# Attention scores as two f32r products of 128 rows each: stacked queries, doubled keys, masks in f32r

## The chip, the cores and the metric

The kernel runs on one core of one Trainium2 chip. The metric is the device time of one execution in microseconds (us), taken from several runs; 2882.18 us is the median of three runs of the kernel before. One more execution was profiled, and every row below comes from it.

## The reference, cut to what matters

Three blocks follow each other on 256 rows of 1024 columns. The first and the third contain attention with 8 query heads of width 64; the second has none. What the change touches is the score of a query row against a key row, which is scaled, masked and put through a softmax:

```python
# first block, branch a (8 key heads), all 256 keys, causal
s_own = jnp.einsum('hqd,hld->hql', qc, k_own)
# first block, branch b (2 key heads): 15 compressed keys, then selected keys, then a window
s = jnp.einsum('grqd,gnd->grqn', qc, kc_b).astype(jnp.float32) * scale
s = jnp.einsum('grqd,gqnld->grqnl', qc, kg).astype(jnp.float32) * scale
s = jnp.einsum('grqd,gkd->grqk', qc, kwc).astype(jnp.float32) * scale
# third block, two layers (2 key heads): window of 128 and 16 meta rows, with a sink
s = jnp.einsum('bnqhgd,bnkhd->bnhgqk', qb, kw, preferred_element_type=jnp.float32) * (HEAD_DIM ** -0.5)
s = jnp.where(mask[None, :, None, None], s, -jnp.inf)
```

With 256 rows the selection and the window of branch b take in every earlier key, so the kernel computes both as causal attention over 256 keys. The layers of the third block see 272 rows in the first layer (16 meta rows are set ahead) and 256 query rows in the second.

## The kernel before, in words

All large products split both operands into a rounded part and a rest, in the type f32r, and add three products (`mm3`, lines 117 to 119): hi by hi, hi by lo, lo by hi. A weight chunk of 128 x 2048 is loaded by SP (`load`, line 108), rounded by ACT into `wh` (line 99) and its rest `wl` is taken by DVE (line 101), two halves each. TensorE (PE) works through these chunks, and the kernel places attention steps between them: `weave` and `gates` run one step of a large product (12 passes of 512 columns) for each step of attention.

Attention (`attend`, line 388) takes the 8 heads in four pairs, (0, 2), (1, 3), (4, 6), (5, 7). In round c it issues the scores of pair c, the product with the values of pair c-2 and the transposes of pair c-1. Queries and keys lie transposed, two heads above each other: head h has rows 64*(h%2) to 64*(h%2)+63 of `qT`. A score is a plain f32 product of 64 rows against 128 or 16 keys (line 409); a causal or window mask is added by a bf16 product of the identity and a mask tile (line 411):

```python
ps = k.tp((128, 2, 256))[:p]
k.pe = nc.tensor.matmul(ps[:, i, f:f + n], q(h), kt, start=True, stop=mask is None)
if mask is not None:
    nc.tensor.matmul(ps[:, i, f:f + n], identb[:p, :p], mask, start=False, stop=True)
```

DVE then takes the maximum (line 412) and ACT the exponential into a tile `P` (line 419), from the tag `w2k`, a ring of nine 2 KB tiles in the first block (`k.w2k, k.pt = 9, 4`, line 474) and of five in the third. `P` is turned by PE (line 428), copied to `PT` by DVE or ACT (lines 432, 434) and multiplied with the values (line 440).

In the first block `attend` runs for branch a (`moba`) and twice for branch b (`branches`), each for two tiles of 128 queries. Tile t=0 has one segment of 128 keys with a mask, t=1 has two segments of which the second has a mask. `cmp_scores` (line 642) adds 8 products of 64 rows against 15 compressed keys for each t (line 650). In the third block each layer has t=0 (128 keys with the causal mask, and the 16 meta keys with a mask), t=1 (two segments of 128 keys, each with a mask), and the first layer also t=2 (16 query rows against 16 keys).

The queries and keys reach `qT`, `kaT`, `kT2` and `kT` by four PE transposes and one ACT copy of 128 x 512 (lines 523, 1469). Between branch a and branch b stands `compress` (line 581), which builds the compressed keys and whose operands come from DVE.

Of the kernel before, what the change touches and what calls it, by code (L numbers as in the profile page):

```python
# [387 lines left out]
def attend(k, pool, p, q, segs, v, identb, sink=None):  # L388
# [10 lines left out]
    ns = [n for _, n, _ in segs(0)]  # L399
# [3 lines left out]
    def scores(c):  # L403
# [3 lines left out]
        for i, h in enumerate(hs):  # L407
            for f, (kt, n, mask) in zip(off, segs(h)):
                k.pe = nc.tensor.matmul(ps[:, i, f:f + n], q(h), kt, start=True, stop=mask is None)  # L409
                if mask is not None:  # L410
                    nc.tensor.matmul(ps[:, i, f:f + n], identb[:p, :p], mask, start=False, stop=True)  # L411
# [59 lines left out]
class Block1:  # L471
    def __init__(self, k, pool):
        self.k, self.pool = k, pool
        k.w2k, k.pt = 9, 4

    def consts(self):
# [7 lines left out]
        self.identb = pool.tile([128, 128], BF16, name="identb")  # L484
        nc.vector.tensor_copy(self.identb, k.ident)
        self.cmask = pool.tile([128, 128], BF16, name="cmask")
        nc.gpsimd.memset(self.cmask, 0.0)
        nc.gpsimd.affine_select(self.cmask, self.cmask, pattern=[[-1, 128]], base=0, channel_multiplier=1,
                                compare_op=OP.is_ge, fill=NEG)
        self.nmask = pool.tile([128, 2, 15], F32, name="nmask")  # L490
# [13 lines left out]
    def tiles(self):  # L504
        p = self.pool
        self.qT = {n: p.tile([128, 4, S], F32, tag="qT" + n, name="qT" + n) for n in "ab"}
        self.kaT = p.tile([128, 4, S], F32, tag="kaT", name="kaT")
        self.kT2 = p.tile([128, 4, S], F32, name="kT2")
        self.va = p.tile([128, 2, 512], F32, name="va")
        self.vs = p.tile([128, 2, 128], F32, name="vs")  # L510
        self.vw = p.tile([128, 2, 128], F32, name="vw")
        self.tT2 = p.tile([128, 4, S], F32, tag="tT2", name="tT2")
        self.gb = p.tile([128, 2, 24], F32, name="gb")
        self.mg = p.tile([128, 2, 2048], F32, name="mg")
        kdp = p.tile([128, 2, 4, 2, 64], F32, tag="kdp", name="kdp")
        self.kdp = [kdp[:, t] for t in range(2)]

    def heads_T(self, src, dst, t):
        k = self.k
        pt = k.tp()  # L520
        for i in range(4):
            k.nc.tensor.transpose(pt[:, i, :], src[:, i * 128:(i + 1) * 128], k.ident)
        k.nc.scalar.copy(dst[:, :, t * 128:(t + 1) * 128], pt)
# [14 lines left out]
    def group(self, j, t, ps):  # L538
        k, nc, pool = self.k, self.k.nc, self.pool
        self.flush(1)  # L540
        if j == 0:
            self.qk(t, ps, "a_q_g", self.qT["a"])
        elif j == 1:
            self.qk(t, ps, "a_k_g", self.kaT)
        elif j == 2:
            nc.scalar.copy(self.va[:, t], ps)
        elif j == 3:
            self.qk(t, ps, "b_q_g", self.qT["b"])
# [15 lines left out]
        else:  # L564
            self.kv2(t, ps[:, 0:128], "b_kw_g", 2)
            nc.scalar.copy(self.vw[:, t], ps[:, 128:256])
            self.heads_T_later(self.kdp[t].rearrange("p c a d -> p (c a d)"), self.kT2, t)
# [5 lines left out]
    def mgate(self, j, t, ps):  # L573
# [3 lines left out]
        m = self.mg[:, t, j * 512:(j + 1) * 512]  # L577
# [3 lines left out]
    def compress(self):  # L581
# [32 lines left out]
        self.kcT = pool.tile([128, 2, 15], F32, name="kcT")  # L614
# [19 lines left out]
        nc.scalar.copy(self.kcT, pt[:, 0:2, 0:15])  # L634

    def attend(self, t, qT, kT, v):
        return attend(self.k, self.pool, 128, lambda h: qT[64 * (h % 2):64 * (h % 2) + 64, h // 2, t * 128:(t + 1) * 128],
                      lambda h: [(kT(h // 2)[64 * (h % 2):64 * (h % 2) + 64, s * 128:(s + 1) * 128], 128,
                                  self.cmask if s == t else None) for s in range(t + 1)],
                      v, self.identb)  # L640

    def cmp_scores(self, t):
# [3 lines left out]
        for q in range(2):  # L646
            ps = k.tp((128, 4, 15))
            r = slice(64 * q, 64 * q + 64)
            for i in range(4):
                nc.tensor.matmul(ps[:, i, :], self.qT["b"][r, i, t * 128:(t + 1) * 128], self.kcT[r, i // 2, :],  # L650
                                 start=True, stop=True)
            nc.vector.tensor_tensor(s.rearrange("p (i q) n -> p q i n", q=2)[:, q], ps,
# [26 lines left out]
    def moba(self, t):  # L679
        k, nc, pool = self.k, self.k.nc, self.pool  # L680
        o, r = yield from self.attend(t, self.qT["a"], lambda hp: self.kaT[:, hp],
# [9 lines left out]
    def branches(self, t):  # L691
# [4 lines left out]
        steps = together(*(self.attend(t, self.qT["b"], lambda hp, i=i: self.kT2[:, 2 * i + hp // 2],  # L696
# [24 lines left out]
    def merge(self):  # L721
        k, nc, pool = self.k, self.k.nc, self.pool
        M = [k.xn() for t in range(2)]
        for h in range(2):
            ch = [k.stream(k.a["w_up_" + n][h, 0]) for n in "ab"]
            c = slice(h * 512, h * 512 + 512)
            for i, n in enumerate("ab"):
                for t in range(2):
# [6 lines left out]
                    gate = self.mg[:, t, i * 1024 + h * 512:i * 1024 + h * 512 + 512]  # L735
# [9 lines left out]
    def run(self):  # L745
# [25 lines left out]
        tags = {"ah": "qTa", "al": "kaT", "bh": "tT2", "bl": "kdp"}  # L771
        yT = lambda n: [pool.tile([128, 4, S], F32R, tag=tags[n + i], name="y" + n + i) for i in "hl"]
        self.yT = {"a": yT("a")}
# [13 lines left out]
        self.yT["b"] = yT("b")  # L787
# [584 lines left out]
class Block3:  # L1372
# [3 lines left out]
    def __init__(self, k, wc):  # L1376
# [10 lines left out]
        self.identb = tl("identb3", [128, 128], BF16)  # L1387
        nc.vector.tensor_copy(self.identb, k.ident)
        self.mask = {}
        for n, base, cm, st, w in (("causal", 0, 1, -1, 128), ("far", -1, -1, 1, 128), ("meta", 111, -1, 1, 16)):  # L1390
            m = self.mask[n] = tl("m" + n, [128, w], BF16)
            nc.gpsimd.memset(m, 0.0)
            nc.gpsimd.affine_select(m, m, pattern=[[st, w]], base=base, channel_multiplier=cm,
                                    compare_op=OP.is_ge, fill=NEG)

# [27 lines left out]
    def meta_cols(self, mt, xx, k0, k1):  # L1423

        self.k.nc.scalar.copy(mt[:, k0:k1, 0:META], xx[:, 0, k0:k1, S:])
        self.k.nc.vector.tensor_copy(mt[:, k0:k1, 32:32 + META], xx[:, 1, k0:k1, S:])
# [26 lines left out]
    def qkv(self, l, pool, nt):  # L1453
# [3 lines left out]
        self.qT = tl("qT", [128, 4, SM])  # L1457
        self.kT = tl("kT", [128, 2, SM])
# [3 lines left out]
        def flush(keep=0):  # L1462

            while len(later) > keep:
                src, n, dst, P = later.pop(0)
# [3 lines left out]
                nc.scalar.copy(dst, pt[:, :n, :P])  # L1469
# [3 lines left out]
        for t in (0, 1, 2):  # L1473
            for j, (w, N) in enumerate(ws):
# [14 lines left out]
                if j == 0:  # L1489
# [3 lines left out]
                    later.append((q.rearrange("p h d -> p (h d)"), 4, self.qT[:, :, o:o + P], P))  # L1493
                else:
# [6 lines left out]
                    later.append((kd.rearrange("p g a d -> p (g a d)"), 2, self.kT[:, :, o:o + P], P))  # L1501
# [3 lines left out]
    def attention(self, l, t, sink, g):  # L1505
# [3 lines left out]
        kt = lambda h, s, n: self.kT[64 * (h % 2):64 * (h % 2) + 64, h // 4, s * 128:s * 128 + n]  # L1509
        M = self.mask  # L1510
        sl = {0: ((0, 128, M["causal"]), (2, 16, M["meta"])),
              1: ((0, 128, M["far"]), (1, 128, M["causal"])),
              2: ((2, 16, M["causal"][:META, :META]),)}[t]
        o, r = yield from attend(k, pool, P, lambda h: self.qT[64 * (h % 2):64 * (h % 2) + 64, h // 2, t * 128:t * 128 + P],
                      lambda h: [(kt(h, s, n), n, m) for s, n, m in sl],
                      lambda s, h: self.v[:sl[s][1], sl[s][0], h // 4 * 64:h // 4 * 64 + 64], self.identb, sink)
# [9 lines left out]
        k.split(self.yy[:, 0, 0:4, c], self.yy[:, 1, 0:4, c], pt[:, :, :P])  # L1526

    def conv(self, l, nt):
# [50 lines left out]
        yield  # L1579
        for cb in range(4):  # L1580
            z = u[:, cb, :n0]
            nc.vector.scalar_tensor_tensor(z, z, self.cg[:, cb:cb + 1], rb, op0=OP.mult, op1=OP.mult)
            k.split(self.yy[:, 0, 4 + cb, :n0], self.yy[:, 1, 4 + cb, :n0], z)
# [46 lines left out]
    def mix(self, l, nt):  # L1630
        k, nc, a = self.k, self.k.nc, self.k.a
        with ExitStack() as ctx:
# [11 lines left out]
            self.yy = pool.tile([128, 2, 8, SM], F32R, name="yy")  # L1644
# [12 lines left out]
            def normalised():  # L1657
                for _ in conv:
                    pass
                if nt == 3:  # L1660
                    self.meta_cols(my, self.yy, 4, 8)
            if nt == 3:
                self.meta_cols(my, self.yy, 0, 4)
            g2, gn = k.row(None, src=a["mix_post_g"][l]), k.row(None, src=a["mlp_pre_g"][l])
            w = a["w3_out"][l]
            yy = lambda c: (self.yy[:, :, 2 * c:2 * c + 2], None if my is None else my[:, 2 * c:2 * c + 2])
# [174 lines left out]
def body(tc, a, out):  # L1841
    with ExitStack() as ctx:
# [6 lines left out]
        with ExitStack() as c:  # L1849
            k.work(c, 2, 2)  # L1850
# [30 lines left out]
```

## Time and profile before

| what | value |
|---|---|
| median of three runs (lowest to highest) | 2882.18 us (2879.19 to 2885.19) |
| the profiled execution's own time | 2877.76 us |
| its span, first to last instruction | 2875.4 us |
| PE busy | 97% of the span |
| DVE, ACT, POOL busy | 61%, 47%, 10% |
| mean granted TensorE clock | 0.978 |

The span is the time from the first to the last instruction on the core; 2.4 us of the execution's own time lie around it. The clock is a share of full speed: it has two levels, 2.4 GHz (1.00) and 1.2 GHz (0.50), so 0.66 over ten us means some 7 us at the lower level. A matmul's recorded duration contains its latency, and passes overlap; the time that a pass takes from the stream is the distance from its start to the start of the next. A plain f32 product leaves two MATMUL records.

### The profile page before, as it was taken

The numbers are of one execution on the slowest core, as the hardware profiler recorded it, in microseconds if no ns is written. First come the engines' busy times: TensorE is split into PE (matmuls) and PEld (weight loads), VectorE is DVE, ScalarE is ACT, GpSimd is POOL, SyncE is SP. The second block draws the span as 40 slices with busy tenths as digits, with TensorE's granted clock in tenths as the row PEclk, the third lists the DMA queues.
The fourth block names the chain that finished last, engine by engine and source line by source line (L and its number), as shares of the span: only waits on it lengthen the run. The fifth ranks groups of instructions, "written<-read, shape, count | busy, mean of one in ns | idle before, by whom it ended". The sixth has DMA issues, their size and how long they took to land. (4 is left out here: it accounts for less than half of the span.)

```text
span 2875.4 us, 44682 instructions
## 1 busy us (share of the span) xinstructions
PE 2779.6 (97%) x18212; PEld 2497.4 (87%) x18212; DVE 1767.7 (61%) x2983; ACT 1351.4 (47%) x2278; POOL 288.8 (10%) x308
## 2 busy tenths in 40 slices
PE   8999979999999999999999999999999999999999
PEld 6787979989999888988799898888988888888897
DVE  6646799775555556548855554766546464464654
ACT  4544445544444555435544444434445354453543
POOL 2101640000000000004300000241001100000100
PEclk9999999999999999999999999999999999998999
DMA  5424437896665555554255555434554234442452
GB/s 205 169 78 148 148 133 261 287 309 217 215 204 202 195 196 203 191 187 152 81 205 190 190 180 188 165 110 162 183 191 163 70 132 161 156 152 74 161 191 103
DMA packets 105982, 496.75 MB, mean 173 GB/s; under 512 B 11040, under 2 KB 44320, under 8 KB 50224
## 3 DMA queue, kind: packets, MB, share of 16 engines
q1 hardware_dynamic: 61632, 443.15, 44.2%
q10 hardware_dynamic: 44144, 50.74, 5.3%
q8 instruction: 143, 2.34, 0.3%
q14 instruction: 63, 0.52, 0.0%
HBM read 476.03 MB, written 17.83 MB: 172 GB/s over the span
## 5 line engine op out<-in xcount | busy, mean ns | idle before, releaser
L101 DVE TENSOR_TENSOR wl<-raw,wh 128x1024 fp32r<-128x1024 f32 x808 | 971.1, 1223 | 636.2 <-ACT wh L99 635.3
L99 ACT CAST wh<-raw 128x1024 fp32r<-128x1024 f32 x848 | 862.1, 1041 | 727.6 <-PE acc L118 239.1
L118 PE MATMUL acc<-xx,wh 128*128 128x256 f32 x1504 | 424.4, 282 | 0.0
L117 PE MATMUL acc<-xx,wh 128*128 128x256 f32 x1504 | 424.0, 282 | 0.0
L119 PE MATMUL acc<-xx,wl 128*128 128x256 f32 x1504 | 423.9, 282 | 0.0
L117 PE MATMUL tp<-xx,wh 128*128 128x256 f32 (+1 forms) x1440 | 410.6, 285 | 5.6 <-ACT ga L970 5.6
L119 PE MATMUL tp<-xx,wl 128*128 128x256 f32 (+1 forms) x1440 | 408.6, 284 | 2.1 <-DVE wl L101 2.1
L118 PE MATMUL tp<-xx,wh 128*128 128x256 f32 (+1 forms) x1440 | 408.5, 284 | 0.0
L117 PEld LDWEIGHTS acc<-xx,wh 128*128 128x128 f32 x1504 | 285.6, 190 | 0.3 <-ACT xs L278 0.3
L119 PEld LDWEIGHTS acc<-xx,wl 128*128 128x128 f32 x1504 | 285.6, 190 | 0.0
L118 PEld LDWEIGHTS acc<-xx,wh 128*128 128x128 f32 x1504 | 283.6, 189 | 0.0
L117 PEld LDWEIGHTS tp<-xx,wh 128*128 128x128 f32 x1440 | 274.0, 190 | 9.1 <-ACT ga L970 6.1
L118 PEld LDWEIGHTS tp<-xx,wh 128*128 128x128 f32 x1440 | 274.2, 190 | 2.4
L119 PEld LDWEIGHTS tp<-xx,wl 128*128 128x128 f32 x1440 | 273.6, 190 | 2.5 <-DVE wl L101 2.5
L117 PE MATMUL acc<-wh,xx 128*128 128x256 f32 (+2 forms) x672 | 226.4, 338 | 3.0 <-ACT xx L112 3.0
L118 PE MATMUL acc<-wl,xx 128*128 128x256 f32 (+2 forms) x672 | 221.9, 331 | 4.1 <-DVE wl L101 4.1
L119 PE MATMUL acc<-wh,xx 128*128 128x256 f32 (+2 forms) x672 | 219.8, 330 | 1.2 <-DVE xx L113 1.2
L147 POOL TENSOR_SCALAR va<-ss 128x1 f32<-128x1 f32 (+1 forms) x49 | 24.5, 500 | 1954.3 <-ACT junk L143 1770.9
L987 PE MATMUL o<-wl,wth 128*128 128x512 f32 x512 | 200.0, 391 | 1.9 <-DVE wl L101 1.9
L986 PE MATMUL o<-wh,wth 128*128 128x512 f32 x512 | 200.6, 392 | 0.0
L989 PE MATMUL o<-wh,wtl 128*128 128x512 f32 x512 | 159.7, 390 | 0.0
L117 PEld LDWEIGHTS acc<-wh,xx 128*128 128x128 f32 x672 | 131.0, 195 | 14.6 <-ACT xx L112 5.0
(483 smaller groups left out, 4817.9 us busy)
## 6 DMA issues: line engine op xcount, KB each, us to landing
raw<-in_ffn_in_dram SPq DMA_DIRECT2D x88, 1024.0 KB, 4.8
raw<-in_peer_u_dram SPq DMA_DIRECT2D x64, 1024.0 KB, 5.0
raw<-in_peer_v_dram SPq DMA_DIRECT2D x64, 1024.0 KB, 4.8
raw<-in_ffn_out_dram SPq DMA_DIRECT2D x44, 1024.0 KB, 4.8
raw<-in_w_up_dram SPq DMA_DIRECT2D x32, 1024.0 KB, 4.8
raw<-in_w_down_dram SPq DMA_DIRECT2D x32, 1024.0 KB, 4.8
gd<-gt ACTq DMA_DIRECT2D x16, 1024.0 KB, 5.5
G<-gd ACTq DMA_DIRECT2D x16, 1024.0 KB, 8.1
```

The costliest lines, as they stand in the source:

```text
L99: nc.scalar.copy(h[:, c], r[:, c])
L101: eng.tensor_tensor(l[:, c], r[:, c], h[:, c].bitcast(F32), op=OP.subtract)
L117: mm(out, ah, bh, start=start, stop=False)
L118: mm(out, ah, bl, start=False, stop=False)
L119: mm(out, al, bh, start=False, stop=stop)
L147: nc.gpsimd.tensor_scalar(v, ss[:, 0:1], EPS, ss[:, 1:2], op0=OP.add, op1=OP.add)
L986: mm(acc[t][h], wh, vh[:, h], start=st, stop=False)
L987: mm(acc[t][h], wh, vl[:, h], start=False, stop=False)
L989: mm(acc[t][h], wl, vh[:, h], start=False, stop=sp)
```

## The change

A query is now kept as hi and lo above each other: `qT` becomes 128 rows x 8 heads, rows 0 to 63 the part rounded to f32r, rows 64 to 127 the rest. The keys stand twice: the tile hi holds the rounded keys in both halves, the tile lo the rest of the keys in rows 0 to 63 and zeros in rows 64 to 127. One pass of 128 rows against hi gives (q_hi + q_lo) by k_hi, one against lo gives q_hi by k_lo. Segments that lie next to each other are one pass: 256 keys at t=1. The masks and the identity become f32r, and the mask passes stand between the pass against hi and the one against lo. The splitting is done when the transposes leave PSUM. To make room, `w2k` goes from 9 to 7 tiles and `pt` from 4 to 3 in the first block, and `mg`, `yT` and, in the third block, half of `yy` move into tiles whose work is over; the ring of 1024-wide gain rows goes from 2 to 1 in the first block.

```diff
+def split_queries(k, pool, Q, pt, c):
+    n = pt.shape[-1]
+    hi = pool.tile([128, 4, 128], F32R, tag="w2k", name="qh", bufs=k.w2k)[:, :, :n]
+    k.nc.scalar.copy(hi, pt)
+    heads = Q.rearrange("p (i e) s -> p e i s", e=2)
+    for e in range(2):
+        r = slice(64 * e, 64 * e + 64)
+        k.nc.vector.tensor_tensor(heads[64:128, e, :, c], pt[r], hi[r].bitcast(F32), op=OP.subtract)
+        k.nc.scalar.copy(heads[0:64, e, :, c], hi[r].bitcast(F32))
+def split_keys(k, hi, lo, pt):
+    k.nc.scalar.copy(hi, pt)
+    k.nc.vector.tensor_tensor(lo[0:64], pt[0:64], hi[0:64].bitcast(F32), op=OP.subtract)
+def score(k, out, Q, hi, lo, mask=None):
+    k.pe = k.nc.tensor.matmul(out, Q, hi, start=True, stop=False)
+    if mask:
+        mask()
+    k.nc.tensor.matmul(out, Q, lo, start=False, stop=True)
...
-            for f, (kt, n, mask) in zip(off, segs(h)):
-                k.pe = nc.tensor.matmul(ps[:, i, f:f + n], q(h), kt, start=True, stop=mask is None)
-                if mask is not None:
-                    nc.tensor.matmul(ps[:, i, f:f + n], identb[:p, :p], mask, start=False, stop=True)
+            f = 0
+            for hi, lo, n in segs(h):
+                def mask():
+                    for at, m in masks:
+                        if f <= at < f + n:
+                            nc.tensor.matmul(ps[:, i, at:at + m.shape[-1]], identr[:p, :p], m, start=False, stop=False)
+                score(k, ps[:, i, f:f + n], Q[:, h, c0], hi, lo, mask)
+                f += n
...
-        k.w2k, k.pt = 9, 4
+        k.w2k, k.pt = 7, 3
...
+        for x in (self.kaL, self.kT2[1]):
+            self.k.nc.gpsimd.memset(x[64:128].bitcast(F32), 0.0)
...
+    def put_ka(self, pt, c):
+        for e in range(2):
+            r, o = slice(64 * e, 64 * e + 64), slice(64 - 64 * e, 128 - 64 * e)
+            k.nc.scalar.copy(hi[r, e, :, c], pt[r])
+            k.nc.scalar.copy(hi[o, e, :, c], pt[r])
+            k.nc.vector.tensor_tensor(lo[0:64, e, :, c], pt[r], hi[r, e, :, c].bitcast(F32), op=OP.subtract)
...
-            ps = k.tp((128, 4, 15))
+            ps = k.tp((128, 4, 16))
             for i in range(4):
-                nc.tensor.matmul(ps[:, i, :], self.qT["b"][r, i, t * 128:(t + 1) * 128], self.kcT[r, i // 2, :],
-                                 start=True, stop=True)
+                score(k, ps[:, i, :], self.qT["b"][:, 2 * i + q, t * 128:t * 128 + 128], *(x[:, i // 2] for x in self.kcT))
...
-            m = self.mask[n] = tl("m" + n, [128, w], BF16)
+            m = wc.tile([128, 128], F32, tag="mask", name="mask")[:, :w]
...
+            self.mask[n] = tl("m" + n, [128, w], F32R)
+            nc.vector.tensor_copy(self.mask[n], m)
...
-        sl = {0: ((0, 128, M["causal"]), (2, 16, M["meta"])),
-              1: ((0, 128, M["far"]), (1, 128, M["causal"])),
-              2: ((2, 16, M["causal"][:META, :META]),)}[t]
+        runs, masks, sl = {0: (((0, 128), (S, META)), ((0, M["causal"]), (128, M["meta"])), ((0, 128), (2, META))),
+                           1: (((0, 256),), ((0, M["far"]), (128, M["causal"])), ((0, 128), (1, 128))),
+                           2: (((S, META),), ((0, M["causal"][:META, :META]),), ((2, META),))}[t]
```

How the instructions stand on the engines, before and after. First PE, in the first block, round 0 of branch a: the four heads whose scores stand ahead of the first woven step (two heads of t=0, two of t=1). `kaT`, `kaH`, `kaL` are the keys, `qTa` the queries, `tp` the scores in PSUM. Before:

```order
L409 MATMUL tp<-kaT,qTa 128x128
L411 LDWEIGHTS identb
L411 MATMUL tp<-cmask,identb 128x128
L409 MATMUL tp<-kaT,qTa 128x128
L411 LDWEIGHTS identb
L411 MATMUL tp<-cmask,identb 128x128
L409 MATMUL tp<-kaT,qTa 128x128 x2
L411 LDWEIGHTS identb
L411 MATMUL tp<-cmask,identb 128x128
L409 MATMUL tp<-kaT,qTa 128x128 x2
L411 LDWEIGHTS identb
L411 MATMUL tp<-cmask,identb 128x128
```

With the change, the same four heads:

```order
L410 MATMUL tp<-kaH,qTa 128x128
L441 MATMUL tp<-cmask,identr 128x128
L413 MATMUL tp<-kaL,qTa 128x128
L410 MATMUL tp<-kaH,qTa 128x128
L441 MATMUL tp<-cmask,identr 128x128
L413 MATMUL tp<-kaL,qTa 128x128
L410 MATMUL tp<-kaH,qTa 128x256
L441 MATMUL tp<-cmask,identr 128x128
L413 MATMUL tp<-kaL,qTa 128x256
L410 MATMUL tp<-kaH,qTa 128x256
L441 MATMUL tp<-cmask,identr 128x128
L413 MATMUL tp<-kaL,qTa 128x256
```

Every head now has three products, two of them 256 columns wide at t=1; the place in PE's order is the same, ahead of the same twelve passes.

Second, PE in the third block, one head of t=0 in the first layer. Before:

```order
L409 MATMUL tp<-kT,qT 128x128
L411 LDWEIGHTS identb_21180
L411 MATMUL tp<-mcausal,identb_21180 128x128
L409 MATMUL tp<-kT,qT 128x16
L411 LDWEIGHTS identb_21180
L411 MATMUL tp<-mmeta,identb_21180 128x16
```

With the change:

```order
L410 MATMUL tp<-kTh,qT 128x128
L441 MATMUL tp<-mcausal,identr 128x128
L413 MATMUL tp<-kTl,qT 128x128
L410 MATMUL tp<-kTh,qT 128x16
L441 MATMUL tp<-mmeta,identr 128x16
L413 MATMUL tp<-kTl,qT 128x16
```

This head has six products, three of them of 16 columns.

Third, DVE between branch a and `compress`, behind the last products of branch a. `hss` and `hn` belong to the norm of the last keys of branch b, `Xs` is an operand of `compress`, `gb` a gate. Before:

```order
L368 TENSOR_REDUCE hss<-xn 128x2
L101 TENSOR_TENSOR wl<-raw,wh 128x1024
L371 TENSOR_TENSOR hn<-acc,qy 128x128
L113 TENSOR_TENSOR Xs<-Xc,Xs 128x480
L372 TENSOR_TENSOR hn<-hn,row 128x128
L570 TENSOR_SCALAR gb<-gb 128x24
```

With the change:

```order
L397 TENSOR_TENSOR qTb<-tp,qh 64x4x128 x2
L368 TENSOR_REDUCE hss<-xn 128x2
L404 TENSOR_TENSOR kT2l<-tp,kT2h 64x4x128
L371 TENSOR_TENSOR hn<-acc,qy 128x128
L113 TENSOR_TENSOR Xs<-Xc,Xs 128x480
L372 TENSOR_TENSOR hn<-hn,row 128x128
L621 TENSOR_SCALAR gb<-gb 128x24
```

Three subtractions of 64 x 512 now stand ahead of `Xs` in DVE's order, and a fourth (`kT2l` of the second tile) further down.

## Rows read from the trace of the kernel before

**Rows 1.** The page: the span, and busy time by engine.

```profile
span 2875.4 us, 44682 instructions
PE 2779.6 (97%) x18212; PEld 2497.4 (87%) x18212; DVE 1767.7 (61%) x2983; ACT 1351.4 (47%) x2278; POOL 288.8 (10%) x308
```

**Rows 2.** Windows, the attention stages: length, busy by engine (instructions), PEclk, DMA, GB/s.

```profile
57.00:224.00 167.00, 160.08 (x970) 130.23 (x969) 97.22 (x215) 79.33 (x192) 9.85 (x14) 0.96 0.33 116
2190.00:2285.00 95.00, 94.81 (x631) 81.52 (x630) 51.81 (x124) 44.12 (x111) 6.12 (x7) 0.93 0.39 137
2550.00:2660.00 110.00, 108.79 (x671) 95.89 (x670) 62.59 (x123) 48.55 (x108) 9.79 (x15) 0.89 0.36 125
```

**Rows 3.** Waits of PE in 2180:2340, the largest: total, times, longest.

```profile
PE tp L205 <- DVE xn L165: 3.5, 2, 1.8
```

**Rows 4.** Timeline of PE, first block: start, duration, line, tiles, shape, count.

```profile
57.51 0.48 PE L409 MATMUL tp<-kaT,qTa 64*128 64x128 f32 x2
...
58.09 0.49 PE L409 MATMUL tp<-kaT,qTa 64*128 64x128 f32 x2
...
58.66 0.71 PE L409 MATMUL tp<-kaT,qTa 64*128 64x128 f32 x4
...
59.46 0.71 PE L409 MATMUL tp<-kaT,qTa 64*128 64x128 f32 x4
```

**Rows 5.** Timeline of PE, compressed scores of the first block.

```profile
179.53 1.20 PE L650 MATMUL tp<-kcT,qTb 64*128 64x15 f32 x13
...
181.12 0.23 PE L411 MATMUL tp<-cmask,identb 128*128 128x128 bf16 x1
```

**Rows 6.** Timeline of PE, third block, masks of t=0 and t=1.

```profile
2235.98 0.23 PE L411 MATMUL tp<-mcausal,identb 128*128 128x128 bf16 x1
...
2237.00 0.23 PE L411 MATMUL tp<-mcausal,identb 128*128 128x128 bf16 x1
...
2266.86 0.23 PE L411 MATMUL tp<-mfar,identb 128*128 128x128 bf16 x1
...
2268.01 0.23 PE L411 MATMUL tp<-mfar,identb 128*128 128x128 bf16 x1
```

**Rows 7.** Timeline of PE: passes of 128, 64 and 256 columns in a stream.

```profile
113.87 1.04 PE L205 MATMUL tp<-ident,ya 128*128 128x128 f32 x8
...
223.01 1.06 PE L440 MATMUL acc<-vw,PT 128*128 128x64 f32 x8
...
2196.10 0.28 PE L117 MATMUL acc<-wh,xx 128*128 128x256 f32 x1
...
2197.16 0.28 PE L117 MATMUL acc<-wh,xx 128*128 128x256 f32 x1
```

**Rows 8.** Windows inside the attention stages, for the clock: columns as in rows 2.

```profile
57.00:100.00 43.00, 43.00 (x256) 34.97 (x255) 23.25 (x58) 20.42 (x58) 5.45 (x8) 1.00 0.28 93
138.00:196.00 58.00, 57.83 (x325) 45.88 (x326) 28.94 (x68) 25.15 (x71) 0.00 (x0) 0.90 0.29 100
2230.00:2260.00 30.00, 30.00 (x170) 26.29 (x171) 11.56 (x30) 8.00 (x28) 0.92 (x2) 0.77 0.21 71
2580.00:2640.00 60.00, 60.00 (x349) 52.35 (x348) 27.07 (x58) 18.82 (x49) 0.79 (x2) 0.80 0.31 106
```

**Rows 9.** Lines 113 and 112: durations in ns (min/median/max), first and last start.

```profile
L113 DVE TENSOR_TENSOR xx<-tp,xx x59: 271/682/693, 12.3 to 2695.2; 128x512 fp32r<-128x512 f32 x56, 128x128 fp32r<-128x128 f32 x3
...
L112 ACT CAST xx<-tp x59: 266/587/600, 11.5 to 2693.7; 128x512 fp32r<-128x512 f32 x56, 128x128 fp32r<-128x128 f32 x3
```

**Rows 10.** Windows where new work may not be covered: columns as in rows 2.

```profile
30.00:60.00 30.00, 27.80 (x126) 21.97 (x124) 20.77 (x34) 13.22 (x20) 6.53 (x6) 0.94 0.49 174
100.00:120.00 20.00, 14.76 (x118) 12.77 (x117) 18.54 (x48) 13.70 (x23) 3.53 (x4) 1.00 0.55 189
```

**Rows 11.** Timeline of DVE and ACT: one pair of heads, maximum to exponential.

```profile
58.77 0.42 DVE L412 TENSOR_REDUCE nm<-tp 128x2 f32<-128x256 f32 x1
...
59.85 0.36 ACT L419 ACTIVATE P<-tp,nm 128x128 f32<-128x128 f32 x1
```

## What the change would do to the time, before it was run

> **What bounds the kernel now.** The page comes first: PE is busy for 97% of the span, DVE for 61%, ACT for 47%, POOL for 10% [rows 1]. That is a mean over stages, so the windows of the three stages with attention are read next [rows 2]. PE is busy for 160.1 of 167 us, 94.8 of 95 and 108.8 of 110; DVE for 55 to 58%, ACT for 44 to 48%. The waits of PE say the same from the other side: the largest of the third block's first attention stage comes to 3.5 us in all, on a norm and not on attention [rows 3]. So PE's stream sets the time here, and a microsecond of score passes saved is a microsecond of the span, as long as DVE and ACT deliver. One more thing stands in rows 2: the granted clock was 0.96, 0.93 and 0.89. With levels of 1.0 and 0.5, the time at the lower one is twice the missing share: 2 x 0.04 x 167 + 2 x 0.07 x 95 + 2 x 0.11 x 110 = 51 us.
>
> The sum is made against the profiled execution, 2877.8 us (span 2875.4 us [rows 1] and 2.4 us around it). It lies 4.4 us, or 0.15%, under the median of 2882.2 us; I take differences from it and set them on the median. A measurement of this kernel can tell about 0.2%, some 5.8 us, from no change: between 2876.4 and 2887.9 us counts as the same.
>
> **The scores before.** The price is the distance between starts. In the first block two heads of t=0 start 0.58 us apart and two of t=1 0.80 us apart [rows 4]. Three attentions of 8 heads make 24 heads for each t: 24 x 0.58 = 13.9 us and 24 x 0.80 = 19.2 us. The compressed scores begin 1.59 us ahead of the next mask; some 0.55 us of that are passes of the next scores, issued between them, so 1.04 us for each t, 2.1 us in all [rows 5]. In the third block equal masks of neighbouring heads are 1.02 us apart at t=0 and 1.15 us at t=1 [rows 6]; two layers make 16 heads for each: 16.3 and 18.4 us. Together 69.9 us at full clock.
>
> **The scores after.** A pass of f32r with 256 columns costs 0.118 us (nine passes from 2196.10 to 2197.16), and a pass in f32 of 128 columns 0.11 us (eight in 1.04 us, less the latency of one) [rows 7]. A pass of 64 columns takes 0.11 us as well [rows 7], so at these widths it isn't the columns that set the distance. No f32r pass of 128 columns stands in this trace. Bounds from its neighbours: half of the 256-column pass below, 0.059 us; two passes of plain f32 above, 0.22 us, since the two more passes of a t=1 head make 0.80 - 0.58 us [rows 4]. I take 0.11 us, the row of equal width and one pass. That gives, head by head:
> - first block, t=0: three passes, 24 x 0.33 = 7.9 us; t=1: two wide and a mask, 24 x (0.236 + 0.11) = 8.3 us;
> - compressed: 32 passes of 16 columns, 3.5 us; here the change loses 1.4 us, as products of the two 64-row halves run beside each other today (13 records in 1.20 us [rows 5]) and no longer do;
> - third block, t=0: six passes, 16 x 0.66 = 10.6 us; t=1: two wide and two masks, 16 x 0.456 = 7.3 us.
>
> Together 37.6 us, so **32.3 us saved**. Part of it is fewer passes; the rest is the delay at each step between 64-row f32 and 128-row bf16, which three-product heads of one shape don't have: two passes and a mask at 0.11 us would be 0.33 us and take 0.58 us [rows 4]. The eight heads of 16 query rows in the third block have three small passes before and after; I set them at nothing.
>
> If a 128-column pass took 0.10 us, 280 passes would save 3 us more; if some of the delay stayed at the steps to the passes around the scores, 5 us less: 27 to 37 us.
>
> **The clock.** Branch a's stretch, 57 to 100 us, runs at 1.00; the losses are at 138 to 196 us (0.90), 2230 to 2260 (0.77) and 2580 to 2640 (0.80) [rows 8], where scores of two attentions stand together. These three hold 49 of the 51 us at the lower level. Work there takes twice its time, so some 25 us is all that the clock could give back. The new scores are little more than half as long, and they are the part of these stretches that changes; but the transposes and products with values (64 and 128 columns at 0.11 us, as slack as before) stay. I take 10 us back, less than half, and 0 to 20 as the bounds: not all can come back while these stay, and below nothing I see no reason, as more of each stretch becomes wide passes.
>
> **What DVE and ACT get.** In the first block each of 2 query sets, 2 tiles gives two subtractions of 64 x 512 and branch a's keys two more for each tile, the doubled keys one: 14. The nearest price is 0.68 us for 128 x 512 (a 64-row one may be no cheaper): 9.5 us of DVE [rows 9]. ACT gets some 14 half copies at up to 0.59 us, 8.3 us [rows 9]. The third block gets about 12 more of each. Against windows at 55 to 58% of DVE and 44 to 48% of ACT [rows 2] this is hidden in the mean. Two places are thin. At 100 to 120 us DVE is busy for 18.5 of 20 us and PE for 14.8 only [rows 10]: four subtractions there, three ahead of the operand that `compress` waits for, come to 2.7 us on the path. At 30 to 60 us DVE has 9.2 us free [rows 10], the eight subtractions of branch a want 5.4 of them: 1 us. The third block's masks now pass one buffer three times, with a cast on DVE between, ahead of the norm that PE already waited 3.5 us for [rows 3]: 1 us. The memsets go to POOL, 10% busy [rows 1], and the smaller rings are the rival below: nothing else. **5 us**, between 0 (all in gaps) and 12 (all 14 subtractions and the masks half in the open).
>
> **The sum.** 2882.2 - 32.3 - 10 + 5 = **2845 us**. Ends: 2882 - 37 - 20 + 0 = 2825 and 2882 - 27 - 0 + 12 = 2867.
>
> **The rivals.**
> - *Narrow f32r passes run like plain f32.* 176 of the new passes have 128 columns: 96 in the first block at t=0, t=1's masks among them, 48 at t=0 and 32 masks at t=1 in the third. At 0.22 instead of 0.11 us they cost 19.4 us more: **2864 us**; with the costs at their upper end 2871. For it: plain f32 takes two passes, and nothing in the trace shows f32r under 256 columns. Against it: at 256 columns f32r takes one pass at 0.118 us. Chance 0.20.
> - *The clock gives nothing back.* The stretches that fell keep their other short passes: **2855 us**. Chance 0.13.
> - *Narrow passes run closer than 0.11 us*, since the same queries are the weights of two passes in a row and their load may be prepared beside the mask: at the middle between 0.059 and 0.11 us, 280 passes of up to 128 columns save 7 us more: **2838 us**. Against it: all of rows 7 under 256 columns stand at 0.11. Chance 0.05. The Trainium skill, page "TensorE: Matmul & The Clock Gate", section "Back-to-back issue gap", gives about 81 ns for each matmul of 128 columns in a sustained stream; by that the sum would be 280 x 0.029 = 8 us lower, and the trace does not agree, as its passes of 128 and of 64 columns stand 110 ns apart [rows 7].
> - *Slower: the ring of tiles becomes the bound.* `w2k` has 7 tiles for 9 in the first block, and the new `qh` takes from it. If the exponential must wait for the transposes of an older `P`, PE gets each round's transposes late by the chain from maximum to exponential, 58.77 to 60.21 us, 1.45 us [rows 11]. With 12 rounds in the first block and 20 in the third, 32 x 1.45 = 46 us, against 32.3 + 10 - 5 = 37 saved: **2891 us**. It decides once more than seven tiles (five in the third block) are wanted at once; two attentions together hold some two `P` each and a finished row, five. Chance 0.04.
> - *The change doesn't do what it says*: steps between row layouts stay, or work in the open takes most of the saving, near **2880 us**. Chance 0.06.
>
> **How the numbers follow.** The forecast has 0.52, the rivals 0.20, 0.13, 0.05, 0.04 and 0.06. All but the last two lie between 2826 and 2872 us; those two hold 0.10, and some of the others' tails the rest of 2 in 10. Faster by over 0.2% are the forecast and the first three rivals but for a tail of the first, 0.88; the same 0.07; slower 0.05, the ring and its like.
>
> **What the profile after would show.** In the first block, starts of scores at t=0 0.33 us apart by head, at t=1 0.35; 0.55 or more would be the first rival. The windows at 138 to 196 us and at the two places of the third block with a clock over 0.90, or unchanged ones for the second. PE's idle time around 100 to 120 us up by some 3 us, its waits on `Xs` and on the third block's norm longer by about 1 us. An ACT exponential waiting on PE's transposes in every round would be the ring. The forecast is wrong if scores with their masks take more than 50 us at full clock, or if the stages are shorter by more than scores and clock explain.

## The result, and the profile after

The kernel with the change takes 2855.28 us at the median of six executions, the kernel before 2879.64 us, at a ratio of 0.9926 with a 95% interval of 0.9910 to 0.9941, so 17 to 26 us less. The 2879.64 us are the median of six executions, three of them those of the first table; the ratio comes out of the other three (2872.94, 2874.50 and 2880.08 us), so it lies nearer to 1 than the quotient of the two medians, 0.9915. One of the six executions of the kernel with the change took 6404.74 us, for a reason that nothing here shows, and is left out of the ratio. The change is faster by more than 0.2%, as forecast. The time is 10 us above the forecast of 2845 us, and of the 37 us that were forecast to go, some 21 by the ratio have gone. The profiled execution fell from a span of 2875.4 to 2851.1 us, by 24.3 us.

The page of the kernel after, its head:

```profile
span 2851.1 us, 44585 instructions
PE 2744.9 (96%) x18132; PEld 2481.8 (87%) x18132; DVE 1786.7 (63%) x3018; ACT 1364.5 (48%) x2302; POOL 294.8 (10%) x314
```

The windows of rows 2 and rows 10 again, with the columns of rows 2:

```profile
57.00:224.00 167.00, 153.32 (x914) 131.63 (x913) 104.88 (x225) 86.33 (x202) 9.41 (x14) 0.91 0.34 118
2190.00:2285.00 95.00, 93.04 (x668) 82.73 (x666) 60.00 (x143) 48.84 (x123) 9.24 (x13) 0.98 0.42 142
2550.00:2660.00 110.00, 104.09 (x693) 94.59 (x692) 70.01 (x139) 54.14 (x114) 13.66 (x17) 0.95 0.38 129
100.00:120.00 20.00, 14.73 (x97) 12.65 (x97) 16.13 (x45) 13.06 (x25) 3.57 (x6) 0.83 0.47 159
30.00:60.00 30.00, 26.34 (x120) 20.56 (x119) 23.58 (x39) 16.91 (x24) 8.21 (x6) 1.00 0.44 161
```

The three attention stages have parted. In the window of the first block PE is busy for 153.3 us instead of 160.1, and that isn't a saving: it stands idle for the rest, and its clock fell from 0.96 to 0.91. In the third block the clock rose from 0.93 and 0.89 to 0.98 and 0.95 [rows 2].

The table divides both spans at the same passes of PE (the 205th, the 3109th and the 3701st of line 118; both kernels have 3872). Scores are counted from the start of each of their passes to the start of the next one on PE, without idle time between the two, and at full clock: time at the lower level counts half. Idle is time in which no pass runs. The clock's part is half the time at the lower level.

| before to after, us | length | scores | PE idle | clock | other passes |
|---|---|---|---|---|---|
| first block | 233.0 to 235.8 | 32.7 to 21.6 | 19.2 to 28.7 | 8.5 to 15.4 | 172.5 to 170.3 |
| between | 1946.9 to 1943.4 | none | 54.1 to 53.3 | 27.3 to 23.9 | 1865.5 to 1866.3 |
| third block | 549.5 to 526.2 | 34.3 to 20.7 | 15.7 to 17.5 | 23.9 to 11.9 | 475.7 to 476.1 |
| end | 146.1 to 145.7 | none | 6.9 to 6.9 | 2.3 to 2.3 | 136.9 to 136.5 |
| sum of the differences | -24.3 | -24.8 | +10.4 | -8.6 | -1.3 |

So the first block spends 11.1 us less on scores and ends 2.8 us later, while the third block gains 23.3 us, more than the 13.6 us that its scores save. These are two single executions, and the clock's part differs between executions of one kernel. An estimate from each execution's span and granted clock (span times the missing share) gives a mean loss to the clock of 58.9 us in 41 executions of the kernel before and of 53.6 us in five with the change: 5 us of gain by the clock, and 17 us by the rest.

The timeline of PE in the kernel after, two heads of t=0 in the first block and what follows them, then a head of t=0 and two of t=1 in the third block:

```profile
73.04 0.33 PE L410 MATMUL tp<-kaH,qTa 128*128 128x128 f32 x1
73.21 0.27 PE L441 MATMUL tp<-cmask,identr 128*128 128x128 f32 x1
73.32 0.28 PE L413 MATMUL tp<-kaL,qTa 128*128 128x128 f32 x1
73.43 0.28 PE L410 MATMUL tp<-kaH,qTa 128*128 128x128 f32 x1
...
73.77 0.61 PE L472 MATMUL acc<-va,PT 128*128 128x64 f32 x4
...
2237.11 0.33 PE L410 MATMUL tp<-kTh,qT 128*128 128x128 f32 x1
...
2237.80 0.31 PE L410 MATMUL tp<-kTh,qT 128*128 128x128 f32 x1
...
2262.97 0.37 PE L410 MATMUL tp<-kTh,qT 128*128 128x256 f32 x1
2263.18 0.23 PE L441 MATMUL tp<-mfar,identr 128*128 128x128 f32 x1
2263.24 0.27 PE L441 MATMUL tp<-mcausal,identr 128*128 128x128 f32 x1
2263.35 0.34 PE L413 MATMUL tp<-kTl,qT 128*128 128x256 f32 x1
2263.52 0.28 PE L410 MATMUL tp<-kTh,qT 128*128 128x256 f32 x1
```

Inside a head the 128-column passes stand 0.11 us apart (73.21, 73.32, 73.43). Behind a 256-column pass one of them takes less, 0.06 us (2263.18 to 2263.24). The heads of the third block take 0.69 us at t=0 (2237.11 to 2237.80) and 0.55 us at t=1 (2262.97 to 2263.52), where 0.66 and 0.46 were forecast, and the pair from 73.04 to 73.77 takes 0.73 us, not 2 x 0.33. The kernel before shows the opposite, a pair within other passes:

```profile
63.10 0.49 PE L409 MATMUL tp<-kaT,qTa 64*128 64x128 f32 x2
...
64.16 0.39 PE L428 MATMUL tp<-ident,P 128*128 128x128 f32 x2
```

1.06 us, not 2 x 0.58: the last mask (at 64.09 us) is left after 0.07 us, as the next pass follows at once.

The new idle time of the first block, 9.4 us, is spread. Counted between the same passes of line 118, 1.2 us of it are added up to the 25th pass, 1.5 up to the 49th, 3.5 up to the 85th (branch a), 2.9 up to the 121st (between branch a and `compress`) and 0.4 behind. In branch a, where the kernel before has no wait of PE at all, PE now waits for the softmax and for a norm; its largest waits in 57:94 of the kernel after:

```profile
PE tp L460 <- ACT P L451: 1.3, 1, 1.3
PE tp L558 <- DVE hn L385: 1.2, 1, 1.2
PE acc L472 <- DVE PT L466: 1.1, 2, 0.9
PE tp L410 <- ACT P L451: 0.8, 1, 0.8
```

Between branch a and `compress` PE waited before as well. The waits in 94:140, before and then after:

```profile
PE acc L117 <- ACT Xs L112: 2.2, 1, 2.2
PE tp L522 <- DVE kdp L536: 2.1, 2, 1.2
PE acc L119 <- DVE Xs L113: 1.0, 2, 0.8
```

```profile
PE tp L558 <- DVE kdp L587: 3.4, 1, 3.4
PE acc L117 <- ACT Xs L112: 2.6, 1, 2.6
PE acc L119 <- DVE Xs L113: 1.4, 2, 1.1
PE tp L205 <- DVE qTb L397: 0.8, 1, 0.8
```

The waits for the keys (`kdp`) and for the split queries (`qTb`), both of DVE, grew by 2.1 us together, those for `Xs` by 0.4 us on ACT and 0.4 on DVE. How late `Xs` is shows in the timeline, the last addition on DVE that it needs and then ACT:

```profile
105.44 0.58 DVE L644 TENSOR_TENSOR Xc<-tT,pos 128x240 f32<-128x240 f32 x1
...
109.91 0.60 ACT L393 CAST qh<-tp 128x512 fp32r<-128x512 f32 x1
...
110.56 1.24 ACT L398 CAST qTb<-qh 64x512 fp32r<-64x512 f32 x2
111.81 0.59 ACT L112 CAST Xs<-Xc 128x480 fp32r<-128x480 f32 x1
```

`Xs` could be cast from 106.0 us on and is cast at 111.8, behind the second tile's queries in ACT's order; its rest on DVE, behind the subtractions, follows at 115.3. Before, ACT waited for the data and cast them at once:

```profile
102.25 0.59 ACT L112 CAST Xs<-Xc 128x480 fp32r<-128x480 f32 x1 [1.12 <-DVE Xc L593]
```

At the very start there is a cost of another kind. The timeline of DVE before, then those of DVE and of POOL in the kernel after:

```profile
8.76 0.88 DVE L165 TENSOR_SCALAR xn<-xn,ya 128x512 f32<-128x512 f32 x2 [1.14 <-POOL ya L150]
```

```profile
8.94 2.51 DVE L165 TENSOR_SCALAR xn<-xn,ya 128x512 f32<-128x512 f32 x2 [1.20 <-POOL ya L150]
11.38 2.35 DVE L101 TENSOR_TENSOR wl<-raw,wh 128x1024 fp32r<-128x1024 f32 x2
...
9.07 2.10 POOL L545 MEMSET kaL<- 64x2048 f32 x1
...
12.70 0.95 POOL L545 MEMSET kT2l<- 64x1024 f32 x1
```

The same two scalings took 0.88 us before; now they take 2.51 us and end soon after POOL's memset of 2.10 us.

### The profile page after: what moved, and what is told of

Read it like the earlier page. It is cut to its first block, busy times and chain, and to the rows that moved or that the text cites. A ratio compares the mean times of both kernels' runs of the same rounds, so it can differ in the third digit from the quotient of the medians.

```text
span 2851.1 us, 44585 instructions
## 1 busy us (share of the span) xinstructions
PE 2744.9 (96%) x18132; PEld 2481.8 (87%) x18132; DVE 1786.7 (63%) x3018; ACT 1364.5 (48%) x2302; POOL 294.8 (10%) x314
## 4 chain that ended last, share of the span: by engine, by line
PE 63%; issue 23%; DVE 7%; POOL 3%; ACT 3%; DMA 1%; POOLq 0%; ACTq 0%; DVEq 0%
PE acc L119 6%; PE acc L117 6%; PE acc L118 6%; PE tp L119 4%; PE tp L117 4%; PE tp L118 4%; PE o L1037 4%; PE o L1036 4%; PE o L1039 4%; PE o L316 2%; PE o L317 2%; PE o L319 2%; DVE wl L101 1%; PE o L1667 1%; PE o L1664 1%
## 5 line engine op out<-in xcount | busy, mean ns | idle before, releaser
L147 POOL TENSOR_SCALAR va<-ss 128x1 f32<-128x1 f32 (+1 forms) x49 | 24.3, 496 | 1949.8 <-ACT junk L143 1768.1
L118 PEld LDWEIGHTS acc<-wl,xx 128*128 128x128 f32 x672 | 132.2, 197 | 16.7 <-DVE wl L101 6.9
```

Of the source, the lines that this page charges most:

```text
L118: mm(out, ah, bl, start=False, stop=False)
```

## The experiments

Each is told against the change as it stands ("the whole change", ratio 0.9926). The intervals of single kernels are some 0.15% wide to either side, about 4 us.

**Which block pays.** The classes of the two blocks, exchanged one at a time for those of the kernel before (the edits in words, as they are long):

```diff
-Block1 and attend of the change          # third_only
+Block1 and attend of the kernel before
-Block3 and attend of the change          # first_only
+Block3 and attend of the kernel before
```

> The third block has the new scores, the first block the old ones. Theory: the whole gain is made in the third block, where the two traces differ by 22 us, and the first block gives its saving back; so this kernel is as fast as the whole change or a little faster, 20 to 25 us under the kernel before, a ratio of 0.991 to 0.993. Rival: both blocks gain by their score passes (9 us in the first, 16 in the third); then this one gains about 16 us, 0.9945.

> The first block has the new scores, the third block the old ones. Theory: the score passes of the first block take 9 us less, and waits of PE (9 us more) and its clock (17 us more at the lower level) take it back: 0 to 4 us slower than the kernel before, ratio 1.000 to 1.0015. Rival, that the first block gains too: about 9 us faster, 0.997.

Third block alone: 2856.42 us, 0.9923 (0.9908 to 0.9937). First block alone: 2876.52 us against 2878.05, 0.9993 (0.9983 to 1.0004), not told apart from the kernel before. All of the gain that can be told from noise is the third block's, as the theory had it. By the estimate from the granted clocks the first block's scores save 6.6 us beside the clock, and the clock takes 4.8 us of them back (twelve executions against 19). The first block's stage with the new scores, in `first_only`, repeats the whole change:

```profile
57.00:100.00 43.00, 39.51 (x226) 33.38 (x226) 26.91 (x58) 24.78 (x62) 4.97 (x6) 0.96 0.28 95
100.00:138.00 38.00, 29.78 (x192) 25.07 (x192) 31.85 (x68) 22.14 (x35) 3.56 (x6) 0.87 0.55 188
138.00:196.00 58.00, 55.95 (x315) 48.11 (x314) 31.16 (x74) 24.32 (x66) 0.87 (x2) 0.88 0.32 111
```

In rows 8 the first of these stretches ran at 1.00, with PE busy for all 43.0 us. It now has 3.5 us of gaps and a clock of 0.96; the second has 8.2 us of gaps and 0.87, where the kernel before had 6.8 us and 1.00:

```profile
100.00:138.00 38.00, 31.25 (x215) 25.81 (x213) 32.21 (x69) 22.38 (x36) 4.40 (x6) 1.00 0.56 204
```

**The price of a narrow pass.**

```diff
-... lambda h: [(*(x[:, :n] for x in kT(h)), n)],
+... lambda h: [(*(x[:, i * 128:i * 128 + 128] for x in kT(h)), 128) for i in range(t + 1)],
...
-1: (((0, 256),), ...
+1: (((0, 128), (128, 128)), ...
```

> The whole change, but 256 adjacent keys are two passes of 128 columns instead of one of 256, for the pass against hi and the one against lo: 80 more passes. If a narrow f32r pass takes 0.11 us, as the timeline of the change shows, 80 x (0.22 - 0.118) = 8 us slower than the whole change, 13 to 17 us under the kernel before (0.994 to 0.9955). If narrow f32r passes cost what plain f32 does, 0.22 us, 80 x (0.44 - 0.118) = 26 us slower, above the kernel before (1.001).

2869.84 us, 0.9971 (0.9960 to 0.9983): some 13 us slower than the whole change. Its timeline settles the pass among passes of its own width:

```profile
60.49 0.27 PE L410 MATMUL tp<-kaH,qTa 128*128 128x128 f32 x1
60.60 0.27 PE L413 MATMUL tp<-kaL,qTa 128*128 128x128 f32 x1
60.71 0.28 PE L410 MATMUL tp<-kaH,qTa 128*128 128x128 f32 x1
```

0.11 us each, half the plain f32 price. Counted as in the table its scores take 50.1 us at full clock instead of 42.2: 7.9 us for the forecast 8. In its profiled execution, 16 us longer than the whole change's, the rest is the clock (13 us more at the lower level, so 6.5 us) and 4 us of idle time, less 3 us of other passes.

**The type of the masks.**

```diff
-self.identr = pool.tile([128, 128], F32R, name="identr")
+self.identr = pool.tile([128, 128], BF16, name="identr")
-self.cmask = pool.tile([128, 128], F32R, name="cmask")
+self.cmask = pool.tile([128, 128], BF16, name="cmask")
...
```

> The whole change, but the masks and the identity are bf16 as before. If the delay of 0.1 us or so at each mask of the kernel before came from the step between 64 and 128 rows, nothing is lost here: within 2 us of the whole change. If it came from the step between the types, 104 masks with a step on either side lose 0.05 to 0.15 us each: 5 to 15 us slower than the whole change.

2847.37 us, 0.9890 (0.9874 to 0.9905): neither theory, it is 0.36% faster than the whole change. The masks' type is a part of the change that costs. A head in the first block, and the identity's weight loads (ns, min/median/max) in this kernel, then in the whole change:

```profile
59.04 0.22 PE L410 MATMUL tp<-kaH,qTa 128*128 128x128 f32 x1
59.10 0.23 PE L441 MATMUL tp<-cmask,identr 128*128 128x128 bf16 x1
59.14 0.31 PE L413 MATMUL tp<-kaL,qTa 128*128 128x128 f32 x1
59.29 0.27 PE L410 MATMUL tp<-kaH,qTa 128*128 128x128 f32 x1
```

```profile
L441 PEld LDWEIGHTS <-identr x120: 80/96/146, 59.1 to 2611.7; 128*128 128x128 bf16 x112, 16*16 16x16 bf16 x8
```

```profile
L441 PEld LDWEIGHTS tp<-cmask,identr x48: 187/190/333, 60.0 to 215.3; 128*128 128x128 f32 x48
```

A mask takes 0.04 us to the start of the next pass where 0.11 stood, and the load is half as long; but the f32r pass behind it takes 0.15 us instead of 0.11 (59.14 to 59.29). The head takes 0.25 us instead of 0.33, so the steps between bf16 and f32r bring no delay of the size that the change removed; that one belongs to the step between 64 and 128 rows, or to plain f32. The rows alone were not tried. Scores fall from 42.2 to 39.3 us at full clock, some 0.03 us for each of the 120 masks; the rest of the gain in the profiled execution is idle time and clock, 1.4 us each. The Trainium skill, page "TensorE: Matmul & The Clock Gate", section "Weight-path perf modes — Fast Weight Load (FWL) and DoubleRow", says that weights of 128 columns load faster when their type is not fp32. The two rows agree, 96 against 190 ns, and put f32r, which the page does not name, on the side of fp32.

**The stall at the start.**

```diff
-        for x in (self.kaL, self.kT2[1]):                     # in tiles
-            self.k.nc.gpsimd.memset(x[64:128].bitcast(F32), 0.0)
...
+        for x in (self.kaL, self.kT2[1]):                     # ahead of pre_norm(0)
+            nc.gpsimd.memset(x[64:128].bitcast(F32), 0.0)     # early_zero; dve_zero: nc.vector.memset
```

> The whole change, but the zeros of the lower halves (kaL 64 x 2048, kT2l 64 x 1024) are written by POOL at the very start, ahead of the first norm, where it stands idle. Theory: in the changed kernel two scalings of the first norm on DVE take 2.51 us instead of 0.88, because POOL fills kaL in the same 2.1 us; with the fill out of the way they take 0.9 us again and everything behind comes 1.6 to 2 us earlier (2853 us). Rival: the scalings are long for another reason; then they stay at 2.5 us and the time at 2855 us.

> The whole change, but the zeros are written by DVE at the very start, where it waits 6 us for the gains; POOL's and PE's order stay. Theory: the scalings of the first norm take 0.88 us in place of 2.51, PE's first product starts 1.6 us earlier and no order is disturbed (as the early fill on POOL disturbed it): 2853 to 2854 us if the clock does the same as before. Rival: the first weights' rests set the start, and nothing moves.

2856.98 us, 0.9931 (0.9918 to 0.9944), and 2856.91 us, 0.9940 (0.9928 to 0.9952): neither is told apart from the whole change. But the cause of the long scalings stands. The scalings in `dve_zero`:

```profile
9.06 0.88 DVE L165 TENSOR_SCALAR xn<-xn,ya 128x512 f32<-128x512 f32 x2 [1.22 <-POOL ya L150]
```

They take 0.88 us in `early_zero` too. There, though, the order on DVE changed, and the scalings came at 12.44 us, behind the weights' rests. In `dve_zero` the order is kept and PE's 25th pass of line 118 comes at 33.2 us instead of 34.9 (32.8 before): 1.7 us, as expected. They are not in the end time; this execution had 12 us more at the lower clock level than the whole change's. By the estimate from the granted clocks both kernels stand 3 us below the whole change beside the clock and lose 5 us more to it. The Trainium skill, page "Advanced Engine Details and Errata", section "Mode Summary", says that DVE's instructions on two ports and GpSimd's block each other: the rows agree, 2.51 against 0.88 us.

**The order between branch a and compress, the work of splitting, and the clock.**

```diff
-        self.flush(1)                                # order
+        self.flush(0 if (j, t) == (4, 1) else 1)
...
-        self.flush()
         ya2 = pool.tile
...
             if i == 0:
+                self.flush()
```

> The whole change, but branch b's second queries are turned and split one step earlier, and its doubled keys only behind the first products of compress. Theory: ACT's queue is what makes the operand Xs late by 6 us between branch a and compress (it stands behind the casts and copies of the queries), with PE idle for 8.2 us of that stage; with it PE's idle time there falls to 3 or 4 us and the kernel is 4 to 6 us faster than the whole change, 2850 us. Rival: PE only waits elsewhere, or the clock falls elsewhere: 2853 to 2857 us.

2854.60 us, 0.9921 (0.9907 to 0.9936). The stage's idle time fell from 8.1 to 5.0 us and the stage from 28.0 to 23.4 us, as the theory said; the kernel's time didn't follow. Its third block, which this edit leaves as it is, had 7 us more at the lower clock level.

```diff
-        return lambda pt, c: split_queries(self.k, self.pool, self.qT[n], pt, c)     # no_rests, first block only
...
+                self.k.nc.scalar.copy(heads[0:64, e, :, c], pt[64 * e:64 * e + 64])
...
-            k.nc.vector.tensor_tensor(lo[0:64, e, :, c], pt[r], hi[r, e, :, c].bitcast(F32), op=OP.subtract)
...
-        split_keys(self.k, *(x[:, :, c] for x in self.kT2), pt)
+        self.k.nc.scalar.copy(self.kT2[0][:, :, c], pt)
...
+            nc.gpsimd.memset(x.bitcast(F32), 0.0)
```

> The whole change, but in the first block the rests of queries and keys are left out (their tiles hold zeros, written at the start), with the copies and subtractions that make them; PE's passes are the same. Theory: the splitting work on DVE and ACT costs the first block its 9 us of new idle time and, by the clock, some of its 17 us at the lower level: 10 to 14 us faster than the whole change, 2841 to 2845 us. Rival: the passes' own form costs it, and the time stays at 2853 to 2855 us.

2851.79 us, 0.9913 (0.9900 to 0.9926): about 4 us where 10 to 14 were expected, not told apart from the whole change. It leaves out the rests of queries and keys, and POOL writes more zeros at the start: PE's 25th pass of line 118 comes at 39.6 us instead of 34.9, and 1.0 us of that is left at the 49th. It too brings the stage between branch a and `compress` to 23.4 us and its idle time to 5.1 us, as it was before the change (5.2). So the splitting makes the new stall there, and its worth in the end time isn't settled. In branch a it changes little: 3.3 us of idle time stay of 3.5, with waits for `P` and `PT`. So most of what PE waits for there is not the splitting; that it is the softmax's chain, which shorter scores no longer cover, is argued and not shown.

```diff
+        fill = k.acc()                               # fill: ahead of the keys' transposes
+        for i in range(12):
+            with k.tc.issue_after(k.pe.ins):
+                nc.tensor.matmul(fill, k.xh[:, i % 8, 0:128], k.xl[:, 0:2, 0:S], start=True, stop=True)
```

> The whole change, and 12 passes of 512 columns that nobody reads, 2.6 us of PE's time at full clock, in PE's order behind the last queries' transposes and ahead of the keys' ones that PE waits 3.4 us for. Theory: the clock's falls at 112.5 to 119.3 and 126.2 to 129.6 us follow from PE's waits between branch a and compress; with the wait filled at least one of them goes and the stage, 28.1 us, gets 2 to 5 us shorter, though PE has more to do. Rival: the falls have nothing to do with the waits: the stage stays at 28 us, or grows by up to 2.6 us. The kernel's time follows only if later falls stay where they are.

2852.20 us, 0.9919 (0.9906 to 0.9932). The stage in the whole change, then with twelve passes more:

```profile
102.80:130.80 28.00, 19.86 (x130) 16.34 (x130) 24.58 (x55) 16.06 (x28) 2.75 (x5) 0.82 0.51 185
```

```profile
101.70:128.60 26.90, 22.05 (x143) 18.75 (x142) 24.54 (x55) 15.93 (x28) 3.16 (x5) 0.87 0.55 192
```

With work added the stage is 1.1 us shorter, less than expected, but not longer: the time at the lower level went from 10 to 7 us, and the wait is filled. That is one execution. But in the five other kernels that leave this stage as it is (`first_only`, `narrow`, `bf16_masks`, `early_zero`, `dve_zero`) it is 10 us each time, and with 5 us of idle time it is 7 in `order`, 3 in `no_rests` and none before the change. So waits bring on part of the falls here; that they bring on all of them is not shown.

**Together.**

> Three edits together on the whole change: masks and identity in bf16, zeros written at the start, the first block's splits reordered. If they add up, 8 + 2 + 5 us: 2840 us, a ratio of 0.9865. If the clock takes back what waits give: 2847 us, as with the bf16 masks alone.

> Masks and identity in bf16, zeros by DVE at the start, the first block's splits reordered. If the parts add up: 2847 - 1.6 - 3 = 2842 to 2843 us; if the clock takes the last two back: 2845 to 2848 us.

> The same with 12 unread passes of 512 columns ahead of the first products of compress. If filling a wait keeps the clock up there: 2 to 4 us under the kernel without them, 2839 to 2841 us; if not, up to 2.6 us over it.

2845.18 us, 0.9886 (0.9872 to 0.9900); 2841.85 us, 0.9884 (0.9869 to 0.9898); 2844.55 us, 0.9894 (0.9879 to 0.9910). All three are faster than the kernel before. The first two are faster than the whole change; the interval of the third meets its interval at 0.9910. None is told apart from bf16 masks alone (0.9890), so that one edit is the one shown to be worth keeping.

## Why the forecast was right, and where it was off

- **The sum.** The sign and the range held. The saving did not come in full: the scores gave 7.5 us less than forecast, idle time took 5.4 more, the clock gave 1.4 us less in the profiled pair and 5 by the mean of the executions.
- **What bounds the kernel.** PE's stream does, in the third block: the scores' saving reaches the end there. In the first block "as long as DVE and ACT deliver" was the condition, and it failed: PE's idle time grew by 9.4 us.
- **The scores.** 32.3 us forecast, 24.8 measured at full clock, a mis-sized term of the right mechanism. The step that failed is the head's price by the distance to its neighbour: scores come in pairs among other passes. Before, that price was 4.8 us too high (69.9 forecast; 67.0 measured, of which 1.9 are the heads of 16 query rows that were set at nothing), as a pair in the first block is 0.1 us shorter than two distances. After, it was 2.6 us too low (37.6 forecast; 42.2 measured, 2.1 of them those heads), as a pair at t=1 takes 0.08 us more in the mean. The price of 0.11 us held for a narrow pass among narrow ones, so the first rival (plain f32's price) falls. The third (under 0.11 us) falls but for a narrow pass behind a wide one, with 0.06 us. With the third falls, for f32r passes among their like, the 81 ns of the Trainium skill, page "TensorE: Matmul & The Clock Gate", section "Back-to-back issue gap".
- **The delay at each mask.** It went, as forecast. But the forecast gave the masks' new type no cost of its own, and it has one: 2.9 us of the stream for the 120 masks against bf16 ones.
- **The clock.** 10 us forecast, 8.6 measured in the profiled pair and 5 by the mean of the executions, and not as told: the third block gets 11.9 us back, the first loses 6.8, and 3.5 come from stretches that the change doesn't touch. The stretch at 138 to 196 us was to rise over 0.90 and stands at 0.88 in `first_only`, 0.88 in the kernel after as well. The second rival's time, 2855 us, is the measured one by luck: the clock gave back a part of what was forecast, and the scores less.
- **What DVE and ACT get.** 5 us forecast, 10.4 us of idle time measured. The place between branch a and `compress` was sized well: 2.7 us forecast, 2.9 measured, though not by DVE alone, as the cast of `Xs` on ACT came 5.8 us behind its data too. The step that failed is the rest of the first block, "hidden in the mean": branch a, with PE busy for all its time before, now has 3.5 us of waits. The memsets on POOL, costed at nothing, stretched DVE's scalings by 1.6 us. The norm ahead of the third block's attention, costed at 1 us more, has shorter waits than before (2.5 us in 2180:2340 instead of 3.5).
- **The slower rival.** The ring of `w2k` didn't bind: in the first block's stage the exponentials wait for `nm` of DVE, for two row sums of DVE (1.1 and 1.0 us), and never for PE's transposes. The largest, from ACT's waits in 57:224 of the kernel after (total, times, longest):

```profile
ACT P L451 <- DVE nm L446: 25.3, 13, 3.9
```

## What to carry to other kernels

Price a short group of passes from its first start to the start of whatever follows it, not by the distance between equal neighbours. When an operand's work moves to another engine, ask what stands behind it in each engine's order: here a cast on ACT that the change did not touch came 5.8 us behind its data. When a stretch in which PE never waits gets shorter, ask which waits come into the open there. And a weight tile that only carries an identity was cheaper here in its 16-bit type.

## What was not expected of the hardware

Two scalings of DVE beside a memset of POOL of 2.10 us took 2.51 instead of 0.88 us, while subtractions with two inputs ran at their usual 1.18 us beside POOL's next memset. And the time at TensorE's lower clock level moved by ten us or more where nothing was edited, between kernels and between executions of one kernel: the six of `order` ran from 2845.88 us at a mean clock of 0.984 to 2859.93 us at 0.980. So edits that save 2 to 5 us in their own stage didn't show in the end time.
